# Hybrid conv/MLA and sparse-attention trunk, two layers: every rounded operand of a product moved to the same place within 128 bytes of its SBUF row

## The chip, the cores and the metric

The kernel runs on one core of a Trainium2 chip. The metric is the device time of one execution in microseconds (us). The kernel before takes 653.75 us as the median of three runs (653.66 to 654.86). Engines are named as in the profile: PE is the matrix engine (TensorE) and PEld its loading of the stationary operand, DVE is VectorE, ACT is ScalarE, POOL is GpSimd, and SP is the engine whose queue starts the DMAs.

## What is computed

The input is one sequence of 256 tokens with 1024 features in float32. Each of the two layers has a mixer and an MLP, each between two RMS norms:

```
for layer in range(2):
    h = rms_norm(x, norm_mix_pre[layer])
    m = mixer_a(h, ...) if layer == 0 else mixer_c(h, ...)
    x = x + rms_norm(m, norm_mix_post[layer])
    h = rms_norm(x, norm_mlp_pre[layer])
    x = x + rms_norm(square(relu(h @ mlp_w1[layer])) @ mlp_w2[layer], norm_mlp_post[layer])
```

`mixer_a` projects h to a gated short convolution (512 channels) and to latent attention with 8 heads, and sends both through one output projection. `mixer_c` is sparse attention with 16 heads in 4 groups and three branches (compressed blocks, selected blocks, a sliding window), mixed by gates, and an output projection. The MLPs go from 1024 to 4096 features and back.

## The kernel before, in words

All data is float32, but most products run in PE's `float32r` format. A float32 operand is split into a rounded part (`hi`) and the rest (`lo`), and a product becomes three matmuls into the same PSUM tile (`mm3`, line 118): x_hi·w_hi, x_hi·w_lo, x_lo·w_hi. The activations are the stationary operand, 128 columns of 512 bytes in each partition. The weights are the moving operand, mostly 512 columns, 2048 bytes in each partition. In the tables below "acc<-whi,xth" is such a matmul: moving `whi`, stationary `xth`, result in the PSUM tile `acc`.

Names of the operands: `whi`/`wlo` are the weights' parts in their usual five buffers, `xhi`/`xlo` the same in three extra buffers that are open between stages (`open_extra`, `close_extra`). `xth`/`xtl` are the transposed, normed residual, `hh`/`hl` the transposed hidden units of the MLP, `cth`/`ctl` the latent q and kv, `mlh`/`mll` and `mch`/`mcl` the mixed outputs in layer 0. In `mixer_c`, `kTh`/`kTl` (moving) and `qT` (stationary) make the scores, and `ptc` with `vcs` the compressed branch.

Weights come as 512 KB chunks (`chunk`): SP starts the DMA to `raw`, ACT (or POOL) rounds to `whi`, DVE subtracts to `wlo`, each in two halves. A chunk feeds 12 matmuls.

PE's order is the order in which the code is written (`manual_schedule`). The first product of an MLP (`w1`) takes, for each of eight column blocks and each of two token halves, 24 matmuls in a row; between two such rows of 24 stand four transposes of the hidden units before (`tr<-ident,hs`, in plain float32). The second product (`two_sided`, both for `w2` and for `mixer_a`'s output projection `a_out`) alternates between the two token halves, six matmuls each, with no transposes until its last chunks. In `mixer_c` a list of filling work (`fills`) stands between the heads' short products.

**Places.** Tiles stand in SBUF in the order in which pools and tiles are opened, so a tile's address is the sum of the sizes ahead of it. Small tiles of 4 to 192 bytes shift all that follows. The tiles of the products are multiples of 512 bytes, with one exception named below, so each has one place within 128 bytes (its address modulo 128), whatever buffer it is in and whatever slice of it is read. The built program gives these places:

```
role        operands                         place before   place after
moving      whi, wlo                              64             0
moving      xhi, xlo                              96             0
stationary  xth, xtl                               0             0
stationary  hh, hl   (MLP, w2)                    64             0
stationary  cth, ctl (mixer_a, latents)           32             0
stationary  mlh, mll, mch, mcl (a_out)            96             0
moving      kTh, kTl, kc, ptc (mixer_c)           96             0
stationary  qT, vcs (mixer_c)                     96             0
moving      c_v0: first slice of a chunk          64             0
moving      c_v0: second slice of a chunk          0            64
```

`c_v0` is the exception: it is 304 columns wide, 1216 bytes, so its second slice stands 64 bytes from the first one's place.

Of the kernel before, what the change touches and what calls it, by code (L numbers as in the profile page):

```python
# [10 lines left out]
F32 = mybir.dt.float32  # L11
# [6 lines left out]
P = 128  # L18
S = 256
# [5 lines left out]
C_HEADS = 16  # L25
# [32 lines left out]
class Trunk:  # L58
# [44 lines left out]
    def mm(self, ps, a, b, start, stop, passes=1):  # L103
        self.nc.tensor.matmul(ps, a, b, start=start, stop=stop)  # L104
        n = 1
        for d in b.shape[1:]:
            n *= d
        self.tick(passes * max(25.0, n / 2.4 + 2.5))
# [10 lines left out]
    def mm3(self, ps, x, w, start, stop):  # L119
        (xh, xl), (wh, wl) = x, w  # L120
        self.mm(ps, xh, wh, start, False)
        self.mm(ps, xh, wl, False, False)
        self.mm(ps, xl, wh, False, stop)
# [9 lines left out]
    def scratch(self, tag):  # L133
        return self.mp.tile([P, 512], F32, name=tag, tag=tag, bufs={"sq": 1, "pst": 2}[tag])

    def trp(self):
        return self.pt.tile([P, 4, P], F32, name="tr", tag="tr", bufs=2)

# [14 lines left out]
        self.xp = self.xs.enter_context(self.pool("extra", side="right"))  # L153

    def close_extra(self):
        self.xs.close()

    def chunk(self, ap, k, n, pool_hi=False, extra=False, first=False):
# [218 lines left out]
    def mixer_a(self, x, rx, fin):  # L377
        nc, A = self.nc, self.A
        with ExitStack() as st:
            lp = st.enter_context(self.pool("la"))  # L380
# [8 lines left out]
            gbs = [lp.tile([P, 512], F32, name=f"gbs{t}") for t in range(2)]  # L389
            rope_t = lp.tile([P, 2, 2, 16], F32, name="rope")  # L390
            mask = lp.tile([P, 256], F32, name="mask")
            uT = lp.tile([P, 4, 2 + S], F32, name="uT")
            cT = [[None, None], [None, None]]
            rq, rkv = [None, None], [None, None]
            nc.gpsimd.memset(uT[:, :, 0:2], 0.0)
# [1 line left out]
            with self.pool("lc") as cpool:  # L397
                cqs = [cpool.tile([P, 768], F32, name=f"cqs{t}") for t in range(2)]
                ckvs = [cpool.tile([P, 256], F32, name=f"ckvs{t}") for t in range(2)]
                cms = [cpool.tile([P, 4], F32, name=f"cms{t}") for t in range(2)]  # L400
                ckvT = [[None], [None]]
                seen = [0]

# [221 lines left out]
    def mixer_c(self, x, rx, fin):  # L625
        nc, A = self.nc, self.A
        with ExitStack() as st:
            lp = st.enter_context(self.pool("ca"))
            pp = st.enter_context(self.pool("caps", space=PSUM))
            cbias = lp.tile([P, 2, C_HEADS, 16], F32, name="cbias")  # L630
            has = lp.tile([P, 2], F32, name="has")
            kTh = lp.tile([P, GRP, 2, 2, P], F32R, name="kTh")
            kTl = lp.tile([P, GRP, 2, 2, P], F32R, name="kTl")
            vv = [lp.tile([P, 4, P], F32, name=f"vv{t}") for t in range(2)]
# [2 lines left out]
            vcs = lp.tile([P, 2, P], F32R, name="vcs")  # L637
            nc.gpsimd.memset(vcs.bitcast(F32), 0.0)
            qT = [[None] * 4 for t in range(2)]
            gates = [lp.tile([P, 3, C_HEADS], F32, name=f"gates{t}") for t in range(2)]  # L640
            rq = [None, None]
            q1cs = []

# [292 lines left out]
            for i in range(len(heads) + LAG + 8):  # L936
                if i < len(heads):
                    gp, g, t, r = heads[i]
# [63 lines left out]
    def start(self, x):  # L1002

        nc, A = self.nc, self.A
        W = A["a_in"]
        cs = []
        warm = self.mp.tile([P, 512], mybir.dt.bfloat16, name="wm")
        nc.vector.memset(warm, 0.0)
        ps = self.trp().rearrange("p a b -> p (a b)")
        for _ in range(WARM):  # L1010
            nc.tensor.matmul(ps, warm[:, 0:P], warm, start=True, stop=True)
        hs, ls = [], []
        for t in range(2):
            for q in range(2):
                x[t][q] = Pairs(hs, t, q), Pairs(ls, t, q)
        with self.pool("init") as ip:
            raw = ip.tile([P, 8, 2, P], F32, name="x0r")

            def part(i):
                sl = slice(2 * i, 2 * i + 2)  # L1020
                nc.sync.dma_start(raw[:, sl], A["xT"][:, sl])
                h, l = self.xt_tile("h"), self.xt_tile("l")
                hs.append(h)
                ls.append(l)
                self.split_scaled_([(h[:, 2 * k:2 * k + 2], l[:, 2 * k:2 * k + 2], raw[:, 2 * i + k],
                                     self.cols[:, 2 * i + k:2 * i + k + 1]) for k in range(2)])
            part(0)
            cs.append(self.chunk(W[0, 0], 2, 512, first=True))
            part(1)
            cs.append(self.chunk(W[0, 1], 2, 512, pool_hi=True))  # L1030
            part(2)
            cs.append(self.chunk(W[0, 2], 2, 512, extra=True))
            part(3)
            cs.append(self.chunk(W[0, 3], 2, 512))
        c2 = []
        for t in range(2):
            c2.append(self.chunk(A["a_c"][0, t], 4, 256, extra=True))
            nc.sync.dma_start(self.X[t], A["x"][t * P:(t + 1) * P, :])
            self.rx0[t] = self.xnorm(t)
        nc.sync.dma_start(self.ident, A["ident"])  # L1040
        nc.scalar.activation(self.ident_r, self.ident, AF.Copy)
        return cs, c2
# [131 lines left out]
```

## Time and profile before

| | |
|---|---|
| median of three runs | 653.75 us (653.66 to 654.86) |
| profiled execution, its own time | 654.89 us |
| profiled execution, span from first to last instruction | 652.9 us |
| PE busy | 638.5 us, 98% of the span |
| DVE, ACT, POOL busy | 417.7, 382.8 and 77.8 us |
| mean granted clock of PE | 0.994 of full speed |

The profiled execution's own time is 2.0 us longer than its span and 1.1 us longer than the median. A matmul's recorded duration reaches into the next one, since PE is pipelined; the step from one start to the next is what a matmul costs in a stream. The timeline gives the starts, and the chain of work that ended last gives whole unbroken streams with their counts.

### The profile page before, as it was taken

Reading aid. Unit: us, or ns where it says so; the run is one execution under the profiler, and the core shown is the slowest. Engines: PE = TensorE matmul, PEld = TensorE weight load, DVE = VectorE, ACT = ScalarE, POOL = GpSimd, SP = SyncE. Lnnn points to the kernel's source line nnn. Section 1 sums busy time; section 2 is a strip of 40 time slices with the busy share of each in tenths; the row PEclk is TensorE's granted clock in tenths of the full one; section 3 lists DMA queues with packets and bytes.
Section 4 is the critical chain, followed back from the end, with each engine's and each line's share of the span. In section 5 each row is a group of like instructions: output and inputs, shape, how many; then the busy total and the mean of one; then the engine's idle time right before and its main releaser. Section 6 shows DMA issues by size and latency. Waiting matters only on the chain.

```text
span 652.9 us, 9401 instructions
## 1 busy us (share of the span) xinstructions
PE 638.5 (98%) x3150; PEld 515.8 (79%) x3150; DVE 417.7 (64%) x963; ACT 382.8 (59%) x866; POOL 77.8 (12%) x135
## 2 busy tenths in 40 slices
PE   8999999999999999999999999999999999999995
PEld 4889877788888888888889876566788888888884
DVE  6668798766657654447748787754965665644443
ACT  4886566746556544446737778765855655644431
POOL 1202340020000000000200155640200000000000
PEclk9999999999999999999999999989999999999998
DMA  8856346545644665556615734012645565655521
GB/s 274 285 188 224 110 123 204 204 141 161 194 162 162 202 212 195 195 184 237 209 34 162 261 102 155 33 65 79 212 141 181 160 192 165 211 194 194 192 79 64
DMA packets 32608, 110.04 MB, mean 169 GB/s; under 512 B 4080, under 2 KB 4656, under 8 KB 32560
## 3 DMA queue, kind: packets, MB, share of 16 engines
q1 hardware_dynamic: 32560, 109.44, 51.3%
q8 instruction: 25, 0.41, 0.3%
q14 instruction: 23, 0.19, 0.1%
HBM read 108.38 MB, written 1.05 MB: 168 GB/s over the span
## 4 chain that ended last, share of the span: by engine, by line
PE 93%; DVE 2%; issue 1%; ACT 1%; DMA 1%; SPq 0%; POOL 0%; DVEq 0%; POOLq 0%; ACTq 0%
PE acc L104 80%; PE tr L111 6%; PE sc L104 5%; DMA raw<-in_a_in 1%; PE tr L116 1%; PE yp L104 1%; ACT pbn L875 1%; DVE xlo L178 0%; DVE wlo L178 0%; ACT pt L899 0%; DVE X L287 0%; POOL rp L147 0%; DVE pbn L873 0%; DVE pst L280 0%; ACT whi L177 0%
## 5 line engine op out<-in xcount | busy, mean ns | idle before, releaser
L178 DVE TENSOR_TENSOR wlo<-raw,whi 128x512 fp32r<-128x512 f32 (+3 forms) x368 | 236.3, 681 | 99.6 <-ACT whi L177 96.4
L177 ACT ACTIVATE whi<-raw 128x512 fp32r<-128x512 f32 (+3 forms) x362 | 205.7, 614 | 106.9 <-PE acc L104 103.2
L104 PE MATMUL acc<-whi,xtl 128*128 128x512 f32 (+3 forms) x416 | 163.5, 393 | 0.0
L104 PE MATMUL acc<-whi,xth 128*128 128x512 f32 (+3 forms) x416 | 161.9, 389 | 0.1
L104 PE MATMUL acc<-wlo,xth 128*128 128x512 f32 (+3 forms) x416 | 160.6, 387 | 1.1 <-DVE wlo L178 1.1
L104 PE MATMUL acc<-whi,hl 128*128 128x512 f32 x256 | 100.0, 391 | 0.0
L104 PE MATMUL acc<-wlo,hh 128*128 128x512 f32 x256 | 99.6, 389 | 0.0
L104 PE MATMUL acc<-whi,hh 128*128 128x512 f32 x256 | 99.6, 389 | 0.0
L104 PEld LDWEIGHTS acc<-whi,xth 128*128 128x128 f32 x416 | 78.5, 189 | 17.4 <-issue 2.8
L104 PEld LDWEIGHTS acc<-wlo,xth 128*128 128x128 f32 x416 | 78.2, 188 | 17.8 <-DVE wlo L178 2.4
L104 PEld LDWEIGHTS acc<-whi,xtl 128*128 128x128 f32 x416 | 78.6, 189 | 14.4
L104 PEld LDWEIGHTS acc<-wlo,hh 128*128 128x128 f32 x256 | 48.1, 188 | 10.0
L104 PEld LDWEIGHTS acc<-whi,hl 128*128 128x128 f32 x256 | 48.1, 188 | 9.9
L104 PEld LDWEIGHTS acc<-whi,hh 128*128 128x128 f32 x256 | 48.1, 188 | 9.8
L147 POOL TENSOR_TENSOR rp<-mse,mhalf 128x1 f32<-128x1 f32 x8 | 4.8, 597 | 405.3 <-DVE mse L144 405.3
L359 ACT ACTIVATE hh<-tr 128x512 fp32r<-128x512 f32 x32 | 19.1, 598 | 48.6 <-PE tr L111 48.6
L360 DVE TENSOR_TENSOR hl<-tr,hh 128x512 fp32r<-128x512 f32 x32 | 22.1, 692 | 38.5 <-ACT hh L359 38.5
L880 POOL TENSOR_SCALAR pbn<-pbn,sm,gates 128x128 f32<-128x128 f32 (+1 forms) x64 | 37.3, 593 | 77.3 <-DVE sm L877 74.5
L351 DVE TENSOR_TENSOR hs<-hr 128x512 f32<-128x512 f32 x32 | 22.0, 688 | 17.3 <-ACT hr L349 17.3
L875 ACT ACTIVATE pbn<-pbn,nm 128x128 f32<-128x128 f32 (+1 forms) x64 | 28.5, 448 | 7.7 <-DVE nm L873 5.9
L349 ACT ACTIVATE hr<-acc,rx 128x512 f32<-128x512 f32 x32 | 22.0, 688 | 18.6 <-PE acc L104 17.4
L873 DVE CUSTOM_DVE_ANT_0 pbn<-sc,bias 128x128 f32<-128x128 f32 (+1 forms) x64 | 21.2, 348 | 3.3 <-PE sc L104 3.0
(234 smaller groups left out, 777.4 us busy)
## 6 DMA issues: line engine op xcount, KB each, us to landing
raw<-in_w SPq DMA_DIRECT2D x128, 512.0 KB, 3.5
raw<-in_c_in SPq DMA_DIRECT2D x16, 512.0 KB, 4.0
raw<-in_a_in SPq DMA_DIRECT2D x15, 512.0 KB, 4.7
raw<-in_a_out SPq DMA_DIRECT2D x8, 512.0 KB, 3.7
raw<-in_c_out SPq DMA_DIRECT2D x8, 512.0 KB, 3.3
raw<-in_a_qup SPq DMA_DIRECT2D x6, 384.0 KB, 3.5
gpost<-in_gpost SPq DMA_DIRECT2D x4, 512.0 KB, 4.8
bias<-in_bias SPq DMA_DIRECT2D x4, 512.0 KB, 5.7
```

The lines of the kernel that those rows point to most:

```text
L104: self.nc.tensor.matmul(ps, a, b, start=start, stop=stop)
L111: self.nc.tensor.transpose(dst, src, self.ident)
L116: self.nc.tensor.transpose(dst.bitcast(F32R), src, self.ident_r)
L177: nc.scalar.activation(hi[:, sl], raw[:, sl], AF.Copy)
L178: nc.vector.tensor_tensor(lo[:, sl], raw[:, sl], hi[:, sl].bitcast(F32), op=OP.subtract)
L349: nc.scalar.activation(r, ps, AF.Relu, scale=self.rxof(rx, t))
L351: nc.vector.tensor_tensor(s, r, r, op=OP.mult)
L359: nc.scalar.activation(h, pt, AF.Copy)
L360: nc.vector.tensor_tensor(l, pt, h.bitcast(F32), op=OP.subtract)
L873: nc.vector.tensor_tensor_reduce(pb[:, sl], sp[:, sl], bias[:, r, 256 - nk:], -1.0, BIG, OP.add, OP.min, nm[:, br:br + 1])
L875: nc.scalar.activation(pb[:, sl], pb[:, sl], AF.Exp, bias=nm[:, br:br + 1], scale=-1.0, accum_out=sm[:, br:br + 1])
L880: nc.gpsimd.tensor_scalar(pb[:, sl], pb[:, sl], sm[:, br:br + 1], gates[t][:, 1 + br, h:h + 1], OP.mult, OP.mult)
```

## The change

Nothing is computed differently. Three pools get a piece of memory that nothing reads or writes (`even`), and five small tiles are rounded up, so that the operands of the table above stand at place 0. The code's numbers of bytes per partition are four times the numbers of elements.

```
+    def even(self, pool, n):
+
+        pool.tile([P, n], F32, name="even")
+
...
     def close_extra(self):
+        self.even(self.xp, 24)
         self.xs.close()
...
-            uT = lp.tile([P, 4, 2 + S], F32, name="uT")
+            uT = lp.tile([P, 4, 8 + S], F32, name="uT")
...
-                cms = [cpool.tile([P, 4], F32, name=f"cms{t}") for t in range(2)]
+                cms = [cpool.tile([P, 32], F32, name=f"cms{t}") for t in range(2)]
...
-            has = lp.tile([P, 2], F32, name="has")
+            has = lp.tile([P, 32], F32, name="has")[:, 0:2]
...
-            gates = [lp.tile([P, 3, C_HEADS], F32, name=f"gates{t}") for t in range(2)]
+            gates = [lp.tile([P, 4, C_HEADS], F32, name=f"gates{t}")[:, 0:3] for t in range(2)]
...
             cs.append(self.chunk(W[0, 3], 2, 512))
         c2 = []
+        self.even(self.mp, 16)
```

On all five engines the built program has the same instructions in the same order as before. What waits for what is the same too, with four exceptions where `mixer_c` begins and takes over memory of the MLP before it: the DMA of `cw1_k` and the clearing of `hv` wait for one matmul later than before, the DMA of `pe_v` into `z_v` for five matmuls later, and the DMA of `w2k`, which stands right behind it on SP and waited for that same matmul, no longer waits for PE.

## Rows read from the trace of the kernel before

**Rows 1.** The page: PE's busy time, and the chain's shares by engine.
```profile
PE 638.5 (98%) x3150; PEld 515.8 (79%) x3150; DVE 417.7 (64%) x963; ACT 382.8 (59%) x866; POOL 77.8 (12%) x135
PE 93%; DVE 2%; issue 1%; ACT 1%; DMA 1%; SPq 0%; POOL 0%; DVEq 0%; POOLq 0%; ACTq 0%
```

**Rows 2.** Groups by shape: count; busy us, mean ns; idle before.
```profile
L104 PE MATMUL acc<-whi,xtl 128*128 128x512 f32 x368 | 149.2, 405 | 0.0
...
L104 PE MATMUL acc<-whi,hl 128*128 128x512 f32 x256 | 100.0, 391 | 0.0
...
L104 PE MATMUL acc<-xhi,xtl 128*128 128x512 f32 x40 | 16.0, 399 | 0.0
...
L104 PE MATMUL acc<-wlo,cth 128*128 128x384 f32 x24 | 8.2, 343 | 0.0
...
L104 PE MATMUL acc<-whi,mcl 128*128 128x512 f32 x16 | 6.5, 406 | 0.0
...
L104 PE MATMUL acc<-whi,ctl 128*128 128x512 f32 x8 | 3.3, 415 | 0.0
```

**Rows 3.** Chain that ended last: start us, length us, engine, line, matmuls.
```profile
104.82 18.43 PE acc L104 x79
...
149.47 5.60 PE acc L104 x24
...
227.82 80.94 PE acc L104 x357
```

**Rows 4.** PE's timeline: start us, recorded us, line, operation.
```profile
11.97 0.39 PE L104 MATMUL acc<-whi,xtl 128*128 128x512 f32 x1
...
223.34 0.40 PE L104 MATMUL acc<-whi,hh 128*128 128x512 f32 x1
...
224.96 0.39 PE L104 MATMUL acc<-wlo,hh 128*128 128x512 f32 x1
...
226.77 0.39 PE L104 MATMUL acc<-whi,hh 128*128 128x512 f32 x1
...
227.90 0.39 PE L104 MATMUL acc<-whi,hh 128*128 128x512 f32 x1
...
228.59 0.39 PE L104 MATMUL acc<-whi,hh 128*128 128x512 f32 x1
...
558.07 0.39 PE L104 MATMUL acc<-whi,xtl 128*128 128x512 f32 x1
```

**Rows 5.** The same, of narrower products (a_qup, then c_v0).
```profile
53.63 0.34 PE L104 MATMUL acc<-wlo,cth 128*128 128x384 f32 x1
...
59.00 0.34 PE L104 MATMUL acc<-whi,ctl 128*128 128x384 f32 x1
...
355.65 0.30 PE L104 MATMUL acc<-whi,xth 128*128 128x304 f32 x1
...
356.07 0.30 PE L104 MATMUL acc<-whi,xth 128*128 128x304 f32 x1
...
356.49 0.39 PE L104 MATMUL acc<-whi,xth 128*128 128x512 f32 x1
```

**Rows 6.** The same, in the attention of layer 1.
```profile
397.51 0.40 PE L104 MATMUL sc<-kTl,qT 128*128 128x512 f32 x1
397.75 0.39 PE L104 MATMUL acc<-ptc,vcs 128*128 128x512 f32 x1
397.98 0.38 PE L111 MATMUL tr<-ident,pbn 128*128 128x128 f32 x2
```

**Rows 7.** Stages: window, length; PE, PEld, DVE, ACT, POOL busy; clock; DMA share; GB/s.
```profile
126.00:223.30 97.30, 97.30 (x455) 78.86 (x454) 63.49 (x113) 57.52 (x110) 3.83 (x3) 1.00 0.52 167
345.00:460.00 115.00, 109.93 (x618) 83.50 (x619) 80.10 (x290) 85.46 (x243) 38.22 (x65) 0.99 0.38 127
426.80:430.20 3.40, 3.40 (x11) 2.70 (x11) 0.96 (x7) 2.12 (x10) 2.99 (x6) 0.50 0.00 0
```

**Rows 8.** Groups by shape on DVE: the subtraction that makes a chunk's lower part.
```profile
L178 DVE TENSOR_TENSOR wlo<-raw,whi 128x512 fp32r<-128x512 f32 x340 | 223.1, 695 | 91.2 <-ACT whi L177 88.1 <-POOL whi L175 1.3
...
L178 DVE TENSOR_TENSOR xlo<-raw,xhi 128x512 fp32r<-128x512 f32 x24 | 15.6, 686 | 4.3 <-ACT xhi L177 4.3
```

## The prediction, written before the changed kernel ran

> **What bounds the kernel now.** I read the page first. PE is busy for 98% of the span, and the chain of work that ended last runs through PE for 93% of it [rows 1]. So a nanosecond off PE's step from one matmul to the next comes off the end, and the other engines matter only where PE waits for them. The second view is the list of groups by shape [rows 2]: the wide split products, 512 columns moving, are the bulk. The group of 368 stands there three times (hi·hi, hi·lo, lo·hi), the group of 40 three times, the group of 16 six times, the groups of 8 six times (three `ct`, three into an `sc` tile): 1104 + 120 + 96 + 48 = 1,368 wide products whose two operands have different places within 128 bytes. Three groups of 256 (`hh`, `hl`) are 768 wide products whose operands have the same place, 64 and 64. The recorded durations (391 to 415 ns) overlap and say little; the steps do.
>
> The third view is the chain in order of time, which gives unbroken streams [rows 3]. The reader should divide. The stream of `a_out` (places 64 and 96) takes 18.43 us for 79 matmuls, 233.3 ns each. A row of 24 in the first product of an MLP (64 and 0) takes 5.60 us, 233.3 ns each. The stream of `w2` (64 and 64) takes 80.94 us for 357, 226.7 ns each. `a_out` and `w2` are written by the same function, feed on the same chunks at the same pace and have no transposes in these stretches; what differs is the stationary tile and its place. The difference of 6.67 ns is what this change can reach.
>
> The fourth view is the timeline where `w2` begins [rows 4]. Equal places are not quick at once: from 223.34 to 224.96 seven steps take 1.62 us, 231 ns each, and only then come eight in 1.81 us, 226 ns each. After the next four transposes the steps from 227.90 to 228.59 are three of 230 ns, and the long stream of 226.7 follows. So a stream settles into the quick step after about four to seven matmuls.
>
> **The change part by part.** It moves no instruction and adds none; it changes addresses, and with them four waits.
>
> *Wide products.* I counted the steps of up to 245 ns between wide products of different places from one start to the next: 1,253, the first and the last as shown [rows 4], together 7.95 us above 226.67 ns each. (The other 115 of the 1,368 precede transposes or stalls, or stand in the first 12 us, and stay as they are.) If every one of them gets the quick step, 7.95 us go. If the first four after each break do not, 1,002 steps remain, worth 6.50 us; if the first seven do not, 805 steps and 5.24 us. I take four, since the breaks here are transposes, as at 227.2 us, and the seven followed other matmuls. Per row of 24 that is 20 x 6.67 = 133 ns of 5.60 us.
>
> *Attention.* Of the 6.50 us, 0.69 lie between 345 and 460 us, where PE is idle for 5.1 of 115 us [rows 7] and the chain passes through ACT and DVE too. I count half of that: 0.35 off. Sum: 6.50 − 0.35 = 6.15 us.
>
> *Narrower split products.* The group of 24 at 384 columns stands three times, 304 and 288 columns (16 each) three times, 256 (16 each) six times: 264. In an unbroken stream of 31 steps from 53.63 to 59.00 us the 384-wide ones take 173.2 ns, which is 13.2 ns over 384 columns at 2.4 GHz [rows 5]. Wide products are 13.4 ns over at equal places and 20.0 ns over at different ones. So the narrow ones, at places 64 and 32, already have the small excess. In `c_v0` both kinds stand side by side: three steps from 355.65 at places 64 and 0 take 0.42 us, the three from 356.07 at places 0 and 0 take 0.42 us too [rows 5]. I count zero; the bounds are zero and 264 x 6.67 = 1.76 us gained.
>
> *Products that were equal at 96 and now are equal at 0* (`kTh`, `kTl`, `ptc`): zero, the relation stays. *The 768 of `hh` and `hl`*, from 64 and 64 to 0 and 0: zero if the relation is what counts; the other case is a rival below.
>
> *The other engines.* DVE's subtraction took 695 ns on `whi` at place 64 and 686 ns on `xhi` at 96 [rows 8], so I price the place at nothing there. PE will ask for chunks 3% sooner in the first product of the MLPs. In 126 to 223 us DVE is busy 63.49 of 97.30 us, ACT 57.52, the DMAs 52% [rows 7]; in `w2` the same chunks already keep up with 226.7 ns. That cover would have to shrink by a third before PE waited.
>
> *The waits.* Three start up to five matmuls later, at most 5 x 0.23 = 1.2 us. `z_v`'s DMA has `w2k` behind it on SP, which waited for that same matmul, and the chain does not name either transfer. Zero, with those 1.2 us as the bound on the loss.
>
> *PE's clock.* From 426.80 to 430.20 us the granted clock is 0.50, 1.2 GHz; PE had idled in the attention just before [rows 7]. It takes up to half of 3.4 us = 1.7 us. Shifted by some microseconds the stretch may vanish or another may come; I count zero and widen the range.
>
> By the profiled execution's own time: 654.89 − 6.15 = 648.7 us. That execution was 1.1 us above the median, so on the median: 653.75 − 6.15 = **647.6 us**.
>
> **The rivals.**
>
> *A. The place is not the cause, or the streams here never settle: no change, 653.75 us.* For it: equal places showed 231 ns for seven steps [rows 4]; two lone products at 96 and 96 took 0.24 and 0.23 us [rows 6]; 304 columns show no difference [rows 5]. If settling took more than 24 matmuls, only the 107 steps beyond the 24th of a stream would gain, 0.7 us, 653.1. Against it: 79 unbroken matmuls of `a_out` never settled [rows 3], while `w2` did within seven and again after its transposes, so within a row of 24 there is room.
>
> A page speaks for A. The Trainium skill, "TensorE: Matmul & The Clock Gate", section "Step-by-step: what each phase is for", says that the moving operand and the weight load have two independent SBUF read ports and that loading the next weights takes nothing from the running matmul; its section "Back-to-back issue gap" gives N/2.4 + 2.5 ns, 215.8 ns for 512 columns, with no term for addresses. By it the time stays at 653.75. The trace disagrees with that figure in both kinds of stream, 226.7 and 233.3.
>
> *B. Slower: it is the place 64 of the stationary operand that makes `w2` quick, not equality.* The trace has one settled stream of equal places, so it can't exclude this. Then the 768 products lose their quick step and the others gain nothing: about 40 of them have no quick step now, so 728 x 6.67 = 4.9 us are lost, 658.6 us. It decides if the long stream of `w2`, at 0 and 0, runs at 233 ns. For it: the pair at 96 and 96 [rows 6]. Against it: those follow transposes by one or two matmuls, where 64 and 64 is not quick either, and three different unequal pairs (64 and 0, 64 and 32, 64 and 96), the fourth being 96 and 0, all behave as one class.
>
> *C. Everything gains*: all 1,253 steps, the narrow ones too: 653.75 − 7.95 − 1.76 = 644.0 us.
>
> **How the numbers follow.** My forecast, including sizes between four settling steps and none, has 0.72; C 0.04; A 0.16; B 0.08. The forecast's own range is 645.3 (7.95 gained, the clock's stretch gone in part) to 649.7 (5.24 gained, 1.2 lost to a wait or the clock). To leave out no more than 2 in 10 the range must reach A, so 645.0 to 654.0; B and C lie outside, with a little of the forecast's own edge. A change of 0.2%, 1.3 us, is about what a measurement of this kernel can tell. Faster by more than that: 0.76; within it: 0.16; slower: 0.08.
>
> **What would show it.** Right: rows of 24 in both first products take about 5.47 us instead of 5.60; `a_out`'s 79 take 17.9 instead of 18.43; the 357 of `w2` still take 80.9; narrower products keep 173 and 140 ns; PE's idle time in the attention grows a little. Wrong: `w2` at 233 ns (B); rows of 24 at 233 ns with `a_out` at 227 (settling is slow); both at 233 (A); the rows of 24 quick but PE waiting for `wlo` or for DMAs (the cover is gone).

## The result, and the profile after

On one chip the kernel before took 654.86 us (653.66 to 655.77, 5 runs) and the changed one 650.45 us (650.22 to 651.75, 5 runs). These are medians; the ratio, here and below, is that of the mean times. It is 0.9942, with a 95% interval of 0.9923 to 0.9960: 3.8 us less, between 2.6 and 5.0. The forecast was 6.15 us less. So the sign and the place were right, and the size was about 60% of what was forecast.

The page of the changed kernel first: its span, the busy times, and the chain's shares by engine.

```profile
span 649.5 us, 9400 instructions
PE 634.2 (98%) x3150; PEld 515.9 (79%) x3150; DVE 417.7 (64%) x963; ACT 383.0 (59%) x866; POOL 77.6 (12%) x135
PE 92%; DVE 3%; ACT 2%; issue 1%; DMA 1%; SPq 0%; POOL 0%; DVEq 0%; POOLq 0%; ACTq 0%
```

Against [rows 1] only PE's busy time moved by more than 0.2 us, from 638.5 to 634.2; the span went from 652.9 to 649.5. Next the chain of the changed kernel in order of time (start us, length us, engine, line, matmuls), to be laid beside [rows 3].

```profile
104.59 18.36 PE acc L104 x79
...
148.93 5.50 PE acc L104 x24
154.87 5.50 PE acc L104 x24
...
220.15 5.50 PE acc L104 x24
226.09 80.97 PE acc L104 x357
...
482.21 5.50 PE acc L104 x24
...
559.38 77.81 PE acc L104 x343
```

Three more lines of the chain before, for the same places:

```profile
155.50 5.60 PE acc L104 x24
...
484.43 5.60 PE acc L104 x24
...
562.78 77.78 PE acc L104 x343
```

The reader should divide again. `w2` still takes 226.8 ns a matmul. A row of 24 fell from 5.60 to 5.50 us, where 5.47 was forecast. `a_out`, for which 17.9 was forecast, stayed at 232.4 ns a matmul: it did not become quick at all. From one row of 24 to the next it is 5.94 us now; before it was 6.03 us, from 149.47 to 155.50. The starts of the two `w2` streams give the whole account: the first moved from 227.82 to 226.09, the second from 562.78 to 559.38, and the end from 652.85 to 649.49. The stretches from the first row of 24 to `w2` lasted 78.35 us in both layers before and last 77.16 and 77.17 now, so these two alone hold 2.37 of the 3.36 us.

Why 5.50 and not 5.47 is seen in PE's timeline of the changed kernel, over one row of 24 (start us, recorded us, line, operation; after four transposes of `hs`).

```profile
154.27 0.60 PE L111 MATMUL tr<-ident,hs 128*128 128x128 f32 x4
154.62 0.48 PE L104 MATMUL acc<-whi,xtl 128*128 128x512 f32 x1
154.94 0.40 PE L104 MATMUL acc<-whi,xth 128*128 128x512 f32 x1
155.18 0.40 PE L104 MATMUL acc<-wlo,xth 128*128 128x512 f32 x1
...
156.80 0.39 PE L104 MATMUL acc<-whi,xtl 128*128 128x512 f32 x1
157.03 0.39 PE L104 MATMUL acc<-whi,xth 128*128 128x512 f32 x1
157.25 0.39 PE L104 MATMUL acc<-wlo,xth 128*128 128x512 f32 x1
...
159.97 0.39 PE L104 MATMUL acc<-wlo,xth 128*128 128x512 f32 x1
```

The first step after the transposes takes 0.32 us. Then nine steps from 154.94 to 157.03 take 2.09 us, 232 ns each, and thirteen from 157.03 to 159.97 take 2.94 us, 226 ns each. The stream does settle, but after ten matmuls, not four (after ten in 16 of the 24 full rows, after eleven in the other 8).

The other engines are as before. Two windows of the changed kernel (length; PE, PEld, DVE, ACT, POOL busy; clock; DMA share; GB/s), for [rows 7]:

```profile
345.00:460.00 115.00, 109.77 (x616) 83.63 (x615) 80.57 (x293) 86.46 (x246) 38.17 (x65) 0.99 0.37 124
...
424.80:428.20 3.40, 3.40 (x11) 2.75 (x11) 0.97 (x7) 2.23 (x10) 2.99 (x6) 0.51 0.00 0
```

PE's idle time in the attention went from 5.07 to 5.23 us, and the stretch at half the clock is still there, 2 us earlier and as long. Executions of one kernel seem to differ by how often such a stretch occurs: the 19 runs of the kernel before that stand beside the experiments on the hidden values lie at 653.2 to 654.1, 655.0 to 655.4 and 657.2 to 657.5 us, with mean granted clocks of 0.997 to 0.999, 0.994 to 0.995 and 0.991 to 0.992, and a ratio of means carries that too, while the two profiled executions here have one such stretch each ahead of the last 10 us, so that their spans, 3.36 us apart, compare like with like. DVE's subtraction on the tiles that moved, by groups of one shape:

```profile
L183 DVE TENSOR_TENSOR wlo<-raw,whi 128x512 fp32r<-128x512 f32 x340 | 223.0, 695 | 89.8 <-ACT whi L182 87.1 <-POOL whi L180 1.3
L183 DVE TENSOR_TENSOR xlo<-raw,xhi 128x512 fp32r<-128x512 f32 x24 | 15.5, 686 | 4.9 <-ACT xhi L182 4.8
```

695 and 686 ns, as in [rows 8]: these moves of address cost DVE nothing.

### The profile page after: what moved, and what is told of

Read it like the earlier page. It is cut to its first block, busy times and chain, and to the rows that moved or that the text cites. A ratio compares the mean times of both kernels' runs of the same rounds, so it can differ in the third digit from the quotient of the medians.

```text
span 649.5 us, 9400 instructions
## 1 busy us (share of the span) xinstructions
PE 634.2 (98%) x3150; PEld 515.9 (79%) x3150; DVE 417.7 (64%) x963; ACT 383.0 (59%) x866; POOL 77.6 (12%) x135
## 4 chain that ended last, share of the span: by engine, by line
PE 92%; DVE 3%; ACT 2%; issue 1%; DMA 1%; SPq 0%; POOL 0%; DVEq 0%; POOLq 0%; ACTq 0%
PE acc L104 79%; PE tr L111 6%; PE sc L104 5%; DVE wlo L183 1%; PE tr L116 1%; DMA raw<-in_a_in 1%; PE yp L104 1%; ACT pbn L880 1%; DVE xtl L258 0%; DVE xlo L183 0%; DVE X L292 0%; POOL rp L151 0%; DVE pst L285 0%; ACT pt L904 0%; ACT sq L283 0%
```

## The experiments

After the result the places were worked out again within 256 bytes (from here on a place is an address modulo 256 unless another number is given), and the classes fell apart as the streams had. (Moving operand of the product first.)

| operands | before | after | step before, after |
|---|---|---|---|
| `whi`/`wlo`, `hh`/`hl` | 192, 192 | 0, 0 | 226.8, 226.9 ns |
| `whi`/`wlo`, `xth`/`xtl` | 192, 0 | 0, 0 | 233.0, 229.3 ns |
| `whi`/`wlo`, `ml` and `mc` | 192, 224 | 0, 128 | 233.3, 232.6 ns |
| `xhi`/`xlo`, `xth`/`xtl` | 224, 0 | 128, 0 | 233.1, 232.6 ns |
| `whi`/`wlo`, `ct` | 192, 32 | 0, 128 | 233.0, 232.5 ns |

(The steps are means over all steps of up to 245 ns between two wide products.) Theory 256 says that a step is quick if both operands have the same place within 256 bytes. Theory 128, that of the prediction, needs another reason for `a_out`. A third is that 512 is the period. The first four kernels ran on one chip, with 653.68 us for the kernel before (17 runs).

**Everything at one place within 512 bytes.** The last three classes of the table join the others.

```
-        self.even(self.xp, 24)
+        self.even(self.xp, 120)
...
+            self.even(lp, 32)
...
-                cms = [cpool.tile([P, 32], F32, name=f"cms{t}") for t in range(2)]
+                cms = [cpool.tile([P, 64], F32, name=f"cms{t}") for t in range(2)]
...
-            has = lp.tile([P, 32], F32, name="has")[:, 0:2]
+            has = lp.tile([P, 128], F32, name="has")[:, 0:2]
```

> Theory (256): a wide product (512 columns) is quick, 226.7 ns a step, when its two operands have the same address modulo 256, not 128; in the changed kernel the weights stand 128 bytes from the mixed outputs and the latents, and the extra weight buffers 128 bytes from the residual. Here all of them stand at the same place modulo 512. Theory: the 79 matmuls of a_out fall from 18.36 to about 17.95 us, the extra buffers' streams go to 226.7 ns, and the time is about 1.2 us below the changed kernel (near 649.2 us, ratio to before 0.990 to 0.993). Rival (128 is the modulus, and a_out does not settle for a reason of its own): a_out stays at 18.36 us and the time at 650.4 us.

649.31 us (649.00 to 650.52, 5 runs), ratio 0.9930 (0.9912 to 0.9948). The chain:

```profile
104.31 17.96 PE acc L104 x79
...
148.17 5.50 PE acc L104 x24
...
225.33 80.97 PE acc L104 x357
```

`a_out` now has 227.3 ns a matmul, as the prediction had wanted it. The rows of 24 stay at 5.50: their ten or eleven slow matmuls have another cause.

**Weights 128 bytes further: equal within 128, unequal within 256.**

```
-        self.even(self.mp, 16)
+        self.even(self.mp, 48)
```

> The changed kernel with the weights and all that is allocated behind them 128 bytes further: still one place modulo 128 for everything, but the weights and the residual are 128 apart modulo 256. Theory (256): the rows of 24 of the first MLP products go back to about 5.6 us, w2 (weights and hidden units moved together) keeps 226.7 ns, and the whole gain is lost: 654 to 655 us, ratio 0.998 to 1.001. Rival (128): rows of 24 stay at 5.50 us, time 650.4 us.

653.96 us (652.83 to 657.09, 12 runs), ratio 1.0002 (0.9988 to 1.0016). The chain:

```profile
105.59 18.42 PE acc L104 x79
...
150.18 5.60 PE acc L104 x24
...
228.52 80.95 PE acc L104 x357
```

The whole gain is gone and the rows of 24 are back at 5.60, though every pair is equal within 128 bytes. `w2`, whose two operands moved together to 128 and 128, stays quick.

**Equal within 256, unequal within 512**: the kernel of the first experiment, with the weights 256 bytes further.

```
-        self.even(self.mp, 16)
+        self.even(self.mp, 80)
```

> As the kernel with one place modulo 512, but weights and all behind them 256 bytes further: weights against the residual equal modulo 256 and different modulo 512; w2 and a_out stay equal modulo 512. Theory (256): as that kernel, about 649.2 us, rows of 24 at 5.50 us. Rival (512 is the modulus): rows of 24 at 5.6 us, time about 653 us, with a_out and w2 quick.

649.98 us (648.85 to 650.77, 5 runs), ratio 0.9937 (0.9918 to 0.9956). The chain:

```profile
104.41 17.96 PE acc L104 x79
...
148.27 5.50 PE acc L104 x24
...
225.44 80.97 PE acc L104 x357
```

Equality within 256 suffices.

**Of the change only the piece in the weights' pool**, in the kernel before:

```
+        self.mp.tile([P, 16], F32, name="even")
         for t in range(2):
             c2.append(self.chunk(A["a_c"][0, t], 4, 256, extra=True))
```

> The kernel before with one part of the change alone: the unused 64 bytes in the main pool ahead of the weights. Weights and hidden units then stand at 0 with the residual; everything else keeps unequal places. Theory (256): this part is the whole change, since the other parts make places equal modulo 128 only: rows of 24 at 5.50 us, time within 0.5 us of the changed kernel (650.4 us, ratio 0.993 to 0.996). Rival (128): the other parts bring about a quarter of the gain, so 651.5 us here.

650.33 us (649.68 to 651.88, 6 runs), ratio 0.9949 (0.9929 to 0.9968). The chain:

```profile
104.72 18.43 PE acc L104 x79
...
149.13 5.50 PE acc L104 x24
...
226.30 80.97 PE acc L104 x357
```

These 64 bytes, which put `whi` and `wlo` where `xth` and `xtl` are, bring the whole of the measured gain, within its interval. The other parts of the change bring nothing that can be told from it.

**MLP's hidden values 128 bytes further**, in the first experiment's kernel: `w2` loses its equality within 256 and keeps it within 128.

```
+            self.even(hp, 32)
```

> On the kernel with one place modulo 512, the MLP's whole pool (hidden units hh and hl, hs) stands 128 bytes further, weights at 0: in w2, the only stage that was quick in the kernel before, operands are equal modulo 128 and unequal modulo 256. Theory (256): w2 goes from 226.7 to about 232.5 ns a step like a_out in the changed kernel; 768 products lose about 5.8 ns, 4.4 us: about 653.7 us, no better than before. Rival (128, and w2 is quick for another reason than the others): w2 stays at 226.7 ns, 649.3 us.

654.62 us (653.39 to 655.76, 10 runs), where the kernel before took 655.07 us (19 runs): ratio 0.9996 (0.9978 to 1.0013). The chain:

```profile
106.68 17.96 PE acc L104 x79
...
150.54 5.50 PE acc L104 x24
...
227.76 82.97 PE acc L104 x357
```

`w2` goes from 226.8 to 232.4 ns a matmul, and the rest keeps its pace. With this the distance is told apart from the place: equal pairs at 192, 0 and 128 were quick, and 0 against 128 was slow in the one direction and in the other.

**Only `hl` 128 bytes further**, same base and chip. Of the three products of a chunk, `whi`·`hl` alone has unequal operands. In the one theory that step is slow; in the other it is the step before it, in which `hl` is loaded beside the running `wlo`·`hh`.

```
-                        l = hp.tile([P, 4, P], F32R, name=f"hl{t}_{j}")
+                        l = hp.tile([P, 640], F32R, name=f"hl{t}_{j}")[:, 32:544].rearrange("p (a b) -> p a b", a=4)
```

> On the kernel with one place modulo 512, the lower part of the hidden units (hl) alone stands 128 bytes further; hh and the weights stay at 0. In w2 the products follow each other as whi-hh, wlo-hh, whi-hl. Own-pair theory (a product is slow when its own two operands differ): only the whi-hl step is slow. Next-load theory (the weight load for the next product is read while this product's columns stream, and it is that pair that must match): only the wlo-hh step, ahead of hl, is slow. Either way one step in three: the stream of 357 takes about 81.6 us and the time is about 650.7 us. Rival (one unequal load keeps the whole stream out of the quick state): every step near 232.5 ns on average, 83.0 us, about 653.7 us.

652.63 us (652.06 to 654.39, 10 runs), ratio 0.9968 (0.9950 to 0.9987). `w2` in the chain:

```profile
225.76 82.50 PE acc L104 x357
```

Both theories missed, and the rival too. Over this stream the steps average 226.7 ns for `whi`·`hh`, 232.7 for `wlo`·`hh` and 234.0 for `whi`·`hl` (their mean, 231.1, is 82.50 us over 357): two of three are slow. So the load of an unequal tile slows the step that it runs beside, which is shown by `wlo`·`hh`, whose own pair is equal. The plainest reading of the third step is that an unequal pair of its own makes a step slow as well; that it is an after-effect of the load one step earlier, no run excludes.

**Where the ten slow matmuls come from.** Four kernels on one chip, all on the first experiment's (653.73 us for the kernel before, 11 runs). A break is the four transposes between two rows. One kernel moves `hs`, which these transposes load, to 192; the other three move the identity, which they multiply by, from 128 to 0, 192 and 64.

```
-                    s = hp.tile([P, 512], F32, name="hs", tag="hs", bufs=3)
+                    s = hp.tile([P, 640], F32, name="hs", tag="hs", bufs=3)[:, 48:560]
```

> What sets the number of slow steps after transposes? In the kernel before, w2 settled after 4 (transposed hs at place 192 modulo 256, identity at 128, products at 192); in the changed kernel it takes 10 (hs 0, identity 128, products 0). Here, on the kernel with one place modulo 512, hs alone moves to 192, products at 0, identity at 128. Theory I (the place of the identity, the moving operand of the transposes, against the products): still 10 slow steps, 649.3 us. Theory H (the place of hs against the identity): 4 slow steps as before, about 38 ns less per break, about 648 us. Rival (other engines draining PSUM cause the slow steps): still 10, here and in every kernel of this batch.

649.09 us (648.90 to 652.87, 6 runs), ratio 0.9926 (0.9902 to 0.9950). All 24 full rows of 24 have ten slow matmuls, where 16 had ten and 8 had eleven in the first experiment's kernel. The place of `hs` does not make the short count.

```
+        self.even(self.cp, 32)
...
+        self.cp.tile([P, 96], F32, name="even2")
```

> As the kernel with one place modulo 512, with the identity of the transposes at 0 modulo 256 instead of 128, like all the products. Theories I and H: about 5 slow steps after the transposes instead of 10 (as in the run with the weights 128 further, where identity, hs and hidden units stood at one place), rows of 24 about 25 ns shorter, 0.5 to 1 us gained, about 648.5 us. Rival: 10 slow steps, 649.3 us.

649.12 us (648.42 to 650.33, 5 runs), ratio 0.9913 (0.9890 to 0.9936). After half of the breaks six matmuls are slow now, after the others ten. With 16 and 112 elements in place of 32 and 96 (identity at 192):

> The identity at 192 modulo 256, products and hs at 0: the identity stands 64 bytes below the products, as in the kernel before in w2. Theories I and H: about 4 slow steps, rows of 24 about 38 ns shorter than with 10, 1 to 1.5 us gained, about 648 us. Rival: 10 slow steps, 649.3 us.

648.49 us (648.18 to 649.34, 4 runs), ratio 0.9910 (0.9887 to 0.9932): four after half of the breaks, ten after the others. Two neighbouring rows in PE's timeline of this kernel:

```profile
147.39 0.60 PE L111 MATMUL tr<-ident,hs 128*128 128x128 f32 x4
...
148.06 0.40 PE L104 MATMUL acc<-whi,xth 128*128 128x512 f32 x1
...
150.15 0.39 PE L104 MATMUL acc<-whi,xth 128*128 128x512 f32 x1
...
153.09 0.39 PE L104 MATMUL acc<-wlo,xth 128*128 128x512 f32 x1
153.32 0.60 PE L111 MATMUL tr<-ident,hs 128*128 128x128 f32 x4
...
154.00 0.39 PE L104 MATMUL acc<-whi,xth 128*128 128x512 f32 x1
...
154.69 0.39 PE L104 MATMUL acc<-whi,xth 128*128 128x512 f32 x1
...
158.99 0.39 PE L104 MATMUL acc<-wlo,xth 128*128 128x512 f32 x1
```

In the first row nine steps from 148.06 to 150.15 take 232 ns each before the quick ones (13 in 2.94 us); in the second only three from 154.00 to 154.69, 230 ns, and then 19 in 4.30 us, 226 ns each. With 48 and 80 elements (identity at 64):

> The identity at 64 modulo 256, products and hs at 0, a distance that no kernel so far had. Theories I and H have no number for it; if the slow steps grow with the distance, some 7 of them and 649 us; if any distance but 128 is good, 4 to 5 and 648 us. Rival: 10, 649.3 us.

650.30 us (648.26 to 651.67, 6 runs), ratio 0.9930 (0.9908 to 0.9952): six, seven and ten, about a third each. Theories I and H and their rival all wanted one number for every break, so none of them holds. In the first twelve steps after the transposes a break costs, above 226.67 ns a step, 136 ns in the first experiment's kernel, 133 with `hs` moved, and 126, 118 and 120 with the identity at 0, 192 and 64. So the identity's place has a part in how long a stream takes to settle, but no place tried makes all breaks short. The steps of all these breaks read like one sequence that is entered at different points: one long break is 314, then 235, 233, 236, 224, 231, 236, 228, 233, 231 and then 227 ns; a short one is 320, then 226, 232, 231 and then 227. The kernel with the identity at 192 has the lowest median of all, but its interval overlaps that of the first experiment: that it beats that kernel is not shown.

## Why the prediction was right in sign and short in size

*The wide products.* Right: PE's step depends on where the two operands lie against each other, and what a step saves comes off the end, since PE sets it. Wrong: the period, which was taken as 128 bytes. The trace of before could not tell: `kTl` with `qT` (224 and 96) and `ptc` with `vcs` (96 and 224) are equal within 128 bytes and unequal within 256, but they follow transposes by a step or two, where steps are slow in any case: in the first experiment's kernel, where these pairs are equal, the steps of `kTl` into the next wide product still take 232 ns (6 of them), as before (6). So their 0.24 us [rows 6] speaks neither for rival A nor for B.

With 256, the products with `ml` and `mc` (`a_out` among them), the `extra` chunks and the latents remain unequal after the change. In the prediction's own count of 1,253 steps, the products with `xth` and `xtl` stood 6.50 us above 226.67 ns a step before (1,026 steps) and 2.86 after; all others went only from 1.45 to 1.32 us (227 steps). The forecast had counted on more: without the first four steps after each break, these others stood 1.27 us above, so 1.1 us of the forecast is missing here. The first experiment brought them 1.0 us in steps, and the weights' shift by 128 bytes showed the period.

*Settling.* The step "I take four" failed. It is ten or eleven in the rows of 24, so a row gains 13 or 14 steps of 6.67, about 90 ns, not 20 x 6.67 = 133; from one row's start to the next it went from 6.03 to 5.94 us. The products that did gain kept 2.86 us where four steps a break would have left 1.27: 1.6 us less. The four rested on the break ahead of `w2`, in the kernel before the only one behind which an equal pair comes. Its trace has that break in both layers and it took four in both, so it gave no warning; the number moves with the identity's place, from four to eleven.

*The sum again.* 6.15 − 1.1 for the period − 1.6 for the settling = 3.4 us, against 3.36 by the spans of the two profiled executions and 3.8 (2.6 to 5.0) by all runs. So the mechanism was right and two terms of the sum were too large. The measured time lies in the range on record, 645.0 to 654.0, because that was widened to reach rival A; the forecast's own range ended at 649.7, and 0.9942 of 653.75 is 650.0.

*Narrower products.* Nearly right. They gain nothing, and lose 0.4 us together: steps of 384 columns go from 173.4 to 176.0 ns (0 against 128 now), of 256 from 117.4 to 119.6, of 288 from 132.3 to 133.2, and only those of 304 fall, from 140.0 to 138.9.

*Attention, DVE, waits, clock.* Right, though the attention swallowed about 0.1 us and not 0.35: its stage, 365.46 to 484.43 us before, lost 0.18 us, and its steps had given 0.31. The 115 us window kept its idle time within 0.2 us, DVE its durations, PE waits for no chunk in the rows of 24 (its window from 148.93 to 226.09 is busy throughout, 77.16 us), and the stretch at half the clock is as long as before. Of the twelve traces of this case four have it there, one has it at 12.8 us, and seven have none ahead of the last 10 us, so it is no mark of the change. The three waits that begin later do not show.

*The rivals.* A, no change, falls with the rows of 24 that settle, and "settling took more than 24" with them: it took ten or eleven. The Trainium skill, "TensorE: Matmul & The Clock Gate", section "Step-by-step: what each phase is for", on which A leaned, says that loading the next tile's weights "doesn't steal SBUF read bandwidth from the running matmul". In this kernel's wide products a load can cost the running matmul time: with `hl` moved, `wlo`·`hh` takes 232.7 ns instead of 226.7 although its own operands are untouched. Whether read bandwidth is what it loses, no run shows. B falls: `w2` is quick at 0 and 0, at 128 and 128 and at 192 and 192. C falls: neither the narrow ones nor the first ten of a stream gain.

Two things stay open: by what mechanism a load or an unequal pair costs the step its 6 ns, and why the settling takes anything from four to eleven. The experiments say on which addresses each depends, and no more.

## What to carry to other kernels

Where PE sets the end and wide rounded products run back to back, compare the places of the moving operand, of its stationary operand and of the one loaded next modulo 256 bytes, and look for a stream that never settles to the shorter step; one unused piece of 64 bytes in the right pool was worth 0.5% here. When a class of rows is explained by a modulus, check whether any pair in the trace could tell it from its double, and hold the forecast open if none can. A gain per instruction in short streams must be counted from the instruction on which it begins, and that count did not carry over from one set of addresses to the next.

## What the runs showed of the hardware that was not expected

A settled 512-column product of this kind takes 226.7 ns from one to the next if the moving operand, the stationary one and the one loaded next have equal places within 256 bytes, and 232 to 234 otherwise, at the distances tried: 128 bytes apart is nearly as slow as 32, 64 or 96. Products of 384 columns or fewer move by 3 ns at most, up or down. After four transposes the short step comes only after four to eleven matmuls, and the place of the identity that the transposes use shifts that number; the place of what they transpose changed it only from ten or eleven to ten.
